# Operands of the delta-rule recurrence made by VectorE and ScalarE, and chunk products placed ahead of the bonus and the pending group norm

## The chip, the cores and the metric

The kernel runs on one core of a Trainium2 chip. The metric is the device time of one execution in microseconds, as the median of its runs. Engines are called PE (TensorE, matmuls), DVE (VectorE), ACT (ScalarE), POOL (GpSimd) and SP (SyncE, which here only issues DMAs). One execution is profiled, and its trace gives each instruction's engine, line, start and duration, and the clock that PE was granted.

## What is computed

One inference step of a hybrid decoder layer, for a prompt of 512 tokens and 8 samples of 4 tokens (together 544 columns), width 2048, in fp32. One input projection feeds three branches: RWKV-7 time mixing with 16 heads of 64, sparse attention over selected keys, and attention into 256 memory tokens. Each branch is gated, and one output projection follows. The change is inside the first branch:

```python
kk = hd(k * k_k)
kk = kk / jnp.maximum(jnp.sqrt(jnp.sum(kk * kk, axis=-1, keepdims=True)), 1e-12)
k = hd(k * (1.0 + (a - 1.0) * k_a))
def step(S, inp):
    r_t, k_t, v_t, w_t, kk_t, a_t = inp
    sa = jnp.einsum('bhvk,bhk->bhv', S, -kk_t)
    S = (S * w_t[:, :, None, :] + sa[..., None] * (kk_t * a_t)[:, :, None, :]
         + v_t[..., None] * k_t[:, :, None, :])
    return S, jnp.einsum('bhvk,bhk->bhv', S, r_t)
S_fin, y = lax.scan(step, wkv0, (r, k, v, decay, kk, a))
y = group_norm(y) * gn_w + gn_b
y = y + jnp.sum(r * k * r_k, axis=-1, keepdims=True) * v
```

Here `decay` and `a` come from two small products (w2, a2), and the last line is the bonus.

## The kernel before, in words

**The whole.** After an RMSNorm the input projection runs as fp32 split in two: each weight block is DMAed by SP (`raw`), ACT makes its rounded high half `wh` (L345) and DVE the rest `wl` (L348), and each product is three matmuls into `ps_acc`, two with `wh` and one with `wl`. These matmuls, 272 columns each, are also the filler that keeps PE busy. Attention comes before and in between. The four groups of the recurrence follow, then the output projection with its own split (L1668, L1669) and the final norm.

**The order of the work.** The kernel is written with priority levels: the recurrence at the main level, the projections of the next group's r, k and v and the gates at a level called "late", side work as "fill". A list scheduler fixes the order of every engine's queue beforehand. On the chip every engine takes its queue in order, so an instruction that waits holds all that stand behind it. The next group's projection is evacuated from PSUM by ACT (L431), DVE (L432) and ACT's copies of a last column (L435, L442), with the token shift applied; `ps_acc` has three buffers. PSUM tags `ps_ts` (tags "tp" and "sc", three buffers), `ps_L` and `ps_c` (one each) serve the recurrence.

**One group** (`rwkv_group`, L1173) holds four heads as two tiles j of 128 rows, each with two halves h of 64. It goes through these stages:

1. *Operands*, for each j (L1194 to L1236): w2 is split in two (ACT L1197, POOL L1198), multiplied (`ps_ts<-wah,w2h` and so on), evacuated (DVE L1206), and put through a sigmoid of three ACT operations (L447 to L449). DVE's scan (L1208) makes the cumulated decay CS; ACT makes PT, SG and CS by exponentials (L1209, L1211, L1212), with POOL's subtraction L1210 between; POOL copies the chunk decays DEC and DS (L1213, L1214). The keys are normalised by a matmul with a block of ones (L1219, DVE L1220, ACT L1221 and L1222, DVE L1223), and L1224, L1225 (DVE) and L1226 (POOL) make the updated key and a·kk. Last, `put` (L1143 for the prompt's 512 columns, L1144 for the samples' 32) writes the products KK·SG, AV·CS and XK·CS on DVE and XR·PT on POOL into the operand tiles LB and BK. In the profile these are called `slots` or `late`, after the pool of 2 KB slots that they lie in.
2. *Bonus* (L1238 to L1246): r·k·r_k (DVE L1241), a matmul with the block of ones into `ps_L`, the product with v (DVE L1245), a DMA to DRAM (`bd`).
3. *Pending norm* (`norm`, L1525 to L1549): the group norm of the group before. Four DVE passes over 128x1024 (L1530, L1531, L1533, L1536), a square and small activations on ACT, transposes, ACT L1544 and four DMAs (`yd`).
4. *Chunk products* (L1255 to L1279): eight times four matmuls BK by LB into `ps_ts`; ACT copies a part (MBT, L1263), DVE masks two (L1264, L1266). SP carries MBT's blocks to DRAM (`md`, L1270) and back in another layout (MB, L1283).
5. *Inversion* (L1287 to L1296): 31 steps of two DVE operations (L1291, L1293) on MB and VB, then a DMA to DRAM (`vd`) and back (TT, L1365). Meanwhile POOL does the samples' own small inversion (`mds`, L1303 to L1316) and scales BK by the chunk decays (L1324, 128x1024 for each j), and PE transposes v and BK (ACT copies L1336, L1346 and on).
6. L1375 transposes 32x32 blocks of TT on DVE, small products complete the inverse, and eight chunks run one after the other (L1468 to L1519).

Of the kernel before, what the change touches and what calls it, by code (L numbers as in the profile page):

```python
# [11 lines left out]
F32 = mybir.dt.float32  # L12
# [5 lines left out]
AF = mybir.ActivationFunctionType  # L18
# [105 lines left out]
def emit(ctx, tc, A):  # L124
# [1021 lines left out]
    def part(t, i, r=slice(0, 128)):  # L1146

        return (t[r, :1024].rearrange("p (n a t) -> p n a t", n=NCH, a=2)[:, :, i],
                t[r, 1024:].rearrange("p (a t) -> p a t", a=2)[:, i])
# [23 lines left out]
    def rwkv_group(g, pending, XK, XV, XR):  # L1173
# [17 lines left out]
        for j in range(2):  # L1191
# [6 lines left out]
            pool.tensor_tensor(W2S[1], w, W2S[0].bitcast(F32), op=OP.subtract)  # L1198
# [11 lines left out]
            pool.tensor_tensor(SG, CS, SG, op=OP.subtract)  # L1210
            act.activation(SG, SG, AF.Exp, scale=-C0)  # L1211
            act.activation(CS, CS, AF.Exp, scale=C0)  # L1212
            pool.tensor_copy(DEC[:, j], PT[:, 63:NPR:64])  # L1213
            pool.tensor_copy(DS[:, j], PT[:, NPR + NT4 - 1:NT:NT4])  # L1214
# [11 lines left out]
            pool.tensor_tensor(AV, AV, KK, op=OP.mult)  # L1226
# [6 lines left out]
            put(XR[:, j], PT, [(HS[h], *part(lb[h], 1, HS[h]), pool) for h in range(2)])  # L1233
# [3 lines left out]

        RK = R([P, 2, NT], name="rk")  # L1238
        bonus = []
        for j in range(2):  # L1240
            dve.scalar_tensor_tensor(RK[:, j], XR[:, j], vec("r_k", 2 * g + j), XK[:, j], op0=OP.mult, op1=OP.mult)  # L1241
            for t0, t1 in HV:
                ps = PS([P, 512], "L")
                bonus.append(mm(ps[:, :t1 - t0], T["bones"], RK[:, j, t0:t1]))
                dve.tensor_tensor(XK[:, j, t0:t1], ps[:, :t1 - t0], XV[:, j, t0:t1], op=OP.mult)  # L1245
        nc.sync.dma_start(BD[g * 256:(g + 1) * 256].rearrange("(j p) t -> p j t", p=P), XK)  # L1246
        F(XK, XR, RK)
        pending()

# [32 lines left out]
        for q in range(2):  # L1282
            nc.sync.dma_start(MB[HS[q]].rearrange("p s t -> p (s t)"), md)  # L1283
        pool.memset(VB, 0.0)
# [37 lines left out]
        for j in range(2):  # L1322
            b4 = BK[j][:, :1024].rearrange("p (n x) -> p n x", n=NCH)
            pool.tensor_tensor(b4, b4, DEC[:, j, :, None].to_broadcast([P, NCH, P]), op=OP.mult)  # L1324
            for a in range(2):
                bs = BK[j][:, 1024 + a * 32:1024 + (a + 1) * 32].rearrange("p (b t) -> p b t", t=NT4)
                pool.tensor_tensor(bs, bs, DS[:, j, :, None].to_broadcast([P, NB, NT4]), op=OP.mult)
# [432 lines left out]
```

## Time and profile before

| what | value |
|---|---|
| median of 3 runs | 1637.25 us (1631.7, 1637.25, 1659.45) |
| the profiled execution | 1635.43 us, span 1633.4 us |
| granted PE clock, mean | 0.967 of full |
| busy: PE, DVE, ACT, POOL | 1538.8, 960.2, 657.4, 400.0 us |
| DMA | 208.19 MB, mean 127 GB/s |
| operand stages to last sample product, groups 0 to 3 | 45.4, 58.8, 58.3, 58.3 us |
| from there to the first L1375, groups 0 to 3 | 46.4, 47.5, 43.3, 50.7 us |

The span is the time from the first to the last instruction of the profile; the execution is 2 us longer. A row of a group of instructions has the line, the engine, the operation, output and inputs with their shapes, the count, then busy time and mean time of one, and the idle time just before with what ended it ("<-ACT lc L435": ACT's instruction of line 435 that wrote `lc`). A stretch has its length, the busy time of each engine, PE's granted clock, the DMA engines' share and GB/s. In a wait, "PE ps_ts L221 <- DVE late L1144: 4.9, 1, 4.9" means that a matmul writing `ps_ts` waited in total 4.9 us, once, for DVE's L1144. All matmuls have the line of their helper, L221 (transposes L227), so they are told apart by tiles.

### The profile page before, as it was taken

To read this page: it belongs to the slowest core of one execution; us is meant where nothing else is said; L and a number is where in the kernel's file an instruction comes from. 1 tells how busy PE (TensorE), PEld (TensorE's weight loads), DVE (VectorE), ACT (ScalarE), POOL (GpSimd) and SP (SyncE) were. 2 spreads that over 40 slices of the span, in tenths; PEclk is the share of its full clock that TensorE was granted. 3 is DMA by queue.
4 is the path that set the end of the run, shared out by engine and by line. 5 is a ranking of instruction groups with operands and counts; after the bars stand their busy time and mean duration, and the time that the engine had idled before them with its cause. 6 is when DMAs were issued, how large, how long until landed. Compare 5 with 4: busy or idle time off the path is not lost. (4 is left out here: it accounts for less than half of the span.)

```text
span 1633.4 us, 31473 instructions
## 1 busy us (share of the span) xinstructions
PE 1538.8 (94%) x12011; PEld 1316.5 (81%) x12011; DVE 960.2 (59%) x2655; ACT 657.4 (40%) x1429; POOL 400.0 (24%) x542
## 2 busy tenths in 40 slices
PE   8999999789888999999999899989998999899997
PEld 6999955789888975678988798879887988777775
DVE  7746677988565642256637763676368645723333
ACT  7556643222133433244335343534353433522223
POOL 0010121120554536224032402241224113201110
PEclk9999999999999999998989898989999999999999
DMA  8733232322786756653412341134213564572233
GB/s 287 218 101 78 75 112 61 93 72 66 227 293 204 232 186 200 204 192 86 111 35 57 79 116 48 49 82 109 58 49 100 140 165 118 162 242 78 84 97 136
DMA packets 241307, 208.19 MB, mean 127 GB/s; under 512 B 45058, under 2 KB 199874, under 8 KB 241156
## 3 DMA queue, kind: packets, MB, share of 16 engines
q1 hardware_dynamic: 227460, 160.03, 34.4%
q0 software_dynamic: 13696, 46.15, 8.9%
q8 instruction: 95, 1.56, 0.4%
q14 instruction: 56, 0.46, 0.1%
HBM read 181.93 MB, written 24.19 MB: 126 GB/s over the span
## 5 line engine op out<-in xcount | busy, mean ns | idle before, releaser
L221 PE MATMUL ps_acc<-xt,wh 128*128 128x272 f32 (+1 forms) x4224 | 873.4, 299 | 13.0 <-ACT lc L435 12.1
L221 PEld LDWEIGHTS ps_acc<-xt,wh 128*128 128x128 f32 (+1 forms) x4224 | 689.0, 192 | 38.3 <-issue 13.9
L221 PE MATMUL ps_acc<-xt,wl 128*128 128x272 f32 (+1 forms) x2112 | 627.9, 297 | 3.0 <-DVE wl L348 3.0
L221 PEld LDWEIGHTS ps_acc<-xt,wl 128*128 128x128 f32 (+1 forms) x2112 | 406.4, 192 | 11.6 <-DVE wl L348 3.9
L345 ACT ACTIVATE wh<-raw 128x512 fp32r<-128x512 f32 (+1 forms) x296 | 185.4, 627 | 312.6 <-PE ps_acc L221 298.1
L348 DVE TENSOR_TENSOR wl<-raw,wh 128x512 fp32r<-128x512 f32 (+1 forms) x285 | 204.6, 719 | 143.3 <-ACT wh L345 142.4
L1669 DVE TENSOR_TENSOR wl<-raw,wh 128x512 fp32r<-128x512 f32 x58 | 43.0, 741 | 108.8 <-ACT wh L1668 97.2
L1668 ACT ACTIVATE wh<-raw 128x512 fp32r<-128x512 f32 x58 | 36.6, 630 | 116.9 <-PE ps_c L221 109.8
L221 PE MATMUL ps_acc<-wh,yt 128*128 128x512 f32 x192 | 63.3, 411 | 3.1 <-DVE late L843 3.1
L470 POOL TENSOR_TENSOR sw<-sw,slots 128x272 f32<-128x272 f32 (+1 forms) x18 | 14.0, 777 | 187.0 <-ACT sw L468 187.0
L221 PEld LDWEIGHTS ps_acc<-wh,yt 128*128 128x128 f32 x192 | 36.3, 193 | 17.5 <-ACT wh L1668 5.9
L221 PE MATMUL ps_ts<-wh,yt 128*128 128x512 f32 x156 | 50.3, 402 | 0.0
L221 PE MATMUL ps_acc<-mt,wh 128*128 128x256 f32 x256 | 48.5, 286 | 0.0
L1620 POOL TENSOR_TENSOR slots<-slots,slots 128x512 f32<-128x512 f32 x11 | 15.3, 1422 | 130.8 <-ACT tm L1618 130.8
L880 POOL DMA_INDIRECT slots<-ck,gix x36 | 37.0, 1028 | 37.3 <-DVE slots L897 22.2
L221 PEld LDWEIGHTS ps_acc<-mt,wh 128*128 128x128 f32 x256 | 40.0, 189 | 0.0
L880 POOL DMA_INDIRECT slots<-cv,gix x32 | 30.5, 954 | 36.7 <-PE ps_L L221 16.0
L221 PE MATMUL ps_ts<-slots,slots 32*32 32x32 f32 (+9 forms) x284 | 38.6, 294 | 0.6 <-DVE slots L739 0.4
L221 PE MATMUL ps_acc<-wl,yt 128*128 128x512 f32 x96 | 38.3, 399 | 0.9 <-DVE wl L1669 0.9
L221 PEld LDWEIGHTS ps_ts<-wh,yt 128*128 128x128 f32 x156 | 28.7, 188 | 12.1 <-ACT wh L1668 5.0
L221 PE MATMUL ps_acc<-mt,wl 128*128 128x256 f32 x128 | 36.7, 287 | 0.4 <-DVE wl L348 0.4
L221 PE MATMUL ps_c<-wh,yt 128*128 128x512 f32 x116 | 37.0, 399 | 0.0
(568 smaller groups left out, 2632.7 us busy)
## 6 DMA issues: line engine op xcount, KB each, us to landing
raw<-w_in SPq DMA_DIRECT2D x260, 256.0 KB, 2.9
raw<-w_out SPq DMA_DIRECT2D x64, 256.0 KB, 3.8
raw<-w_mem SPq DMA_DIRECT2D x32, 256.0 KB, 4.0
slots<-xp SPq DMA_DIRECT2D x16, 512.0 KB, 6.7
slots<-qd POOLq DMA_DIRECT2D x8, 512.0 KB, 5.6
late<-qd POOLq DMA_DIRECT2D x8, 512.0 KB, 6.0
o_y<-slots SPq DMA_DIRECT2D x8, 512.0 KB, 3.5
slots<-yd SPq DMA_DIRECT2D x7, 544.0 KB, 4.0
```

The source lines that it names most:

```text
L221: return pe.matmul(out, lhsT=lhsT, rhs=rhs, start=start, stop=stop, **kw)
L345: splits.append(act.activation(wh[:, :, :m], raw[:, :, :m], AF.Copy))
L348: eng.tensor_tensor(wl[:, :, :m], raw[:, :, :m], wh[:, :, :m].bitcast(F32), op=OP.subtract)
L470: pool.tensor_tensor(sw[:np_], sw[:np_], sin[:np_, t0:t1], op=OP.mult)
L880: pool.indirect_dma_start(out=dst[:, u], out_offset=None, in_=src, in_offset=bass.IndirectOffsetOnAxis(ap=GIX[:, 2 * q + u:2 * q + u + 1], ...
L1620: pool.tensor_tensor(z, z, nw[g // 2][:, g % 2 * 512:(g % 2 + 1) * 512], op=OP.mult)
L1668: act.activation(wh, raw, AF.Copy)
L1669: dve.tensor_tensor(wl, raw, wh.bitcast(F32), op=OP.subtract)
```

## The change

It has four parts. (1) Operations of the operand stage go from POOL to DVE: w2's low half (L1198), L1210, L1226, and the XR·PT put. (2) The two small copies DEC and DS go from POOL to ACT. (3) The bonus and the call of the pending norm move from before the chunk products to behind the issue of the MB loads; the bonus matmuls take turns in `ps_L` and `ps_c`, where they all had `ps_L`. VB's memsets follow them. (4) The scaling of BK by the chunk decay goes from one POOL operation on 128x1024 for each j to eight ACT activations on 128x128, each with its chunk's decay as a per-row scale (L1323 of the changed kernel). Lines from L1238 to L1270 move up or down by the shift: the product's copy and masks L1263, L1264, L1266 become L1250, L1251, L1253, the bonus L1241 and L1245 become L1274 and L1278, L1324 becomes L1323, and the lines behind, L1375 and the norm among them, lose 1.

```diff
--- before.py
+++ after.py
@@ -1195,7 +1195,7 @@
             W2S = [S([P, P], F32R, tag="w2" + t, bufs=1) for t in "hl"]
             w = W2A2[:, j * P:(j + 1) * P]
             act.activation(W2S[0], w, AF.Copy)
-            pool.tensor_tensor(W2S[1], w, W2S[0].bitcast(F32), op=OP.subtract)
+            dve.tensor_tensor(W2S[1], w, W2S[0].bitcast(F32), op=OP.subtract)
             SG, AV, CS, PT, KK, RN = t1[:, 0], t1[:, 1], t2[:, 0], t2[:, 1], t3[:, 0], t3[:, 1]
             for t0, t1_ in HV:
                 pss = [PS([P, 512], "sc") for _ in range(2)]
@@ -1207,11 +1207,11 @@
             sigmoid_(flat(t1))
             dve.tensor_tensor_scan(CS, T["scanm"], SG, 0.0, op0=OP.mult, op1=OP.add)
             act.activation(PT, CS, AF.Exp, scale=-C0)
-            pool.tensor_tensor(SG, CS, SG, op=OP.subtract)
+            dve.tensor_tensor(SG, CS, SG, op=OP.subtract)
             act.activation(SG, SG, AF.Exp, scale=-C0)
             act.activation(CS, CS, AF.Exp, scale=C0)
-            pool.tensor_copy(DEC[:, j], PT[:, 63:NPR:64])
-            pool.tensor_copy(DS[:, j], PT[:, NPR + NT4 - 1:NT:NT4])
+            act.copy(DEC[:, j], PT[:, 63:NPR:64])
+            act.copy(DS[:, j], PT[:, NPR + NT4 - 1:NT:NT4])
 
             act.activation(RN, XK[:, j], AF.Square, scale=vec("k_k", c))
             for t0, t1_ in HV:
@@ -1223,30 +1223,17 @@
             dve.scalar_tensor_tensor(KK, XK[:, j], vec("k_k", c), RN, op0=OP.mult, op1=OP.mult)
             dve.tensor_scalar(RN, AV, vec("k_a", c), OMKA[:, c:c + 1], op0=OP.mult, op1=OP.add)
             dve.tensor_tensor(XK[:, j], XK[:, j], RN, op=OP.mult)
-            pool.tensor_tensor(AV, AV, KK, op=OP.mult)
+            dve.tensor_tensor(AV, AV, KK, op=OP.mult)
 
             lb = [R([P, 1088], name="lb") for _ in range(2)]
             bk = R([P, 1088], name="bk")
             put(KK, SG, [(HS[h], *part(lb[h], 0, HS[h]), dve) for h in range(2)])
             put(AV, CS, [(slice(0, 128), *part(bk, 0), dve)])
             put(XK[:, j], CS, [(slice(0, 128), *part(bk, 1), dve)])
-            put(XR[:, j], PT, [(HS[h], *part(lb[h], 1, HS[h]), pool) for h in range(2)])
+            put(XR[:, j], PT, [(HS[h], *part(lb[h], 1, HS[h]), dve) for h in range(2)])
             F(t1, t2, t3)
             LB.append(lb)
             BK.append(bk)
-
-        RK = R([P, 2, NT], name="rk")
-        bonus = []
-        for j in range(2):
-            dve.scalar_tensor_tensor(RK[:, j], XR[:, j], vec("r_k", 2 * g + j), XK[:, j], op0=OP.mult, op1=OP.mult)
-            for t0, t1 in HV:
-                ps = PS([P, 512], "L")
-                bonus.append(mm(ps[:, :t1 - t0], T["bones"], RK[:, j, t0:t1]))
-                dve.tensor_tensor(XK[:, j, t0:t1], ps[:, :t1 - t0], XV[:, j, t0:t1], op=OP.mult)
-        nc.sync.dma_start(BD[g * 256:(g + 1) * 256].rearrange("(j p) t -> p j t", p=P), XK)
-        F(XK, XR, RK)
-        pending()
-
 
         AB = R([P, 2, NCH, 64], name="ab")
         MBT = R([P, 2, NCH, 64], name="mbt")
@@ -1281,6 +1268,17 @@
         MB, VB = R([P, 32, 32], name="mb"), R([P, 16, 32], name="vb")
         for q in range(2):
             nc.sync.dma_start(MB[HS[q]].rearrange("p s t -> p (s t)"), md)
+
+        RK = R([P, 2, NT], name="rk")
+        for j in range(2):
+            dve.scalar_tensor_tensor(RK[:, j], XR[:, j], vec("r_k", 2 * g + j), XK[:, j], op0=OP.mult, op1=OP.mult)
+            for (t0, t1), tag in zip(HV, "Lc"):
+                ps = PS([P, 512], tag)
+                mm(ps[:, :t1 - t0], T["bones"], RK[:, j, t0:t1])
+                dve.tensor_tensor(XK[:, j, t0:t1], ps[:, :t1 - t0], XV[:, j, t0:t1], op=OP.mult)
+        nc.sync.dma_start(BD[g * 256:(g + 1) * 256].rearrange("(j p) t -> p j t", p=P), XK)
+        F(XK, XR, RK)
+        pending()
         pool.memset(VB, 0.0)
         for q in range(2):
             pool.memset(fv(VB[HS[q]], [[34, 16]], q), -1.0)
@@ -1320,8 +1318,9 @@
 
 
         for j in range(2):
-            b4 = BK[j][:, :1024].rearrange("p (n x) -> p n x", n=NCH)
-            pool.tensor_tensor(b4, b4, DEC[:, j, :, None].to_broadcast([P, NCH, P]), op=OP.mult)
+            for n in range(NCH):
+                b = BK[j][:, n * P:(n + 1) * P]
+                act.activation(b, b, AF.Copy, scale=DEC[:, j, n:n + 1])
             for a in range(2):
                 bs = BK[j][:, 1024 + a * 32:1024 + (a + 1) * 32].rearrange("p (b t) -> p b t", t=NT4)
                 pool.tensor_tensor(bs, bs, DS[:, j, :, None].to_broadcast([P, NB, NT4]), op=OP.mult)
```

The order of three queues, in group 1. First DVE, just ahead of the first chunk product's masks, before (L1241 and L1245 are the bonus, L1533 and L1536 the norm, L348 the fill weights' split, L847 a gate):

```order
L1241 SCALAR_TENSOR_TENSOR late_2643<-slots_73,vecs,slots_72 128x544
L1245 TENSOR_TENSOR slots_72<-ps_L,slots_74 128x272
L847 TENSOR_TENSOR slots_72<-slots_72 128x544
L1245 TENSOR_TENSOR slots_72<-ps_L,slots_74 128x272
L348 TENSOR_TENSOR wl<-raw,wh 128x512
L1533 TENSOR_REDUCE gst<-late_2643 128x16
L1536 TENSOR_TENSOR slots_74<-slots_74,gst 128x1024
L348 TENSOR_TENSOR wl<-raw,wh 128x512
L1264 TENSOR_TENSOR slots_72<-ps_ts,cmain 64x256
L1266 TENSOR_TENSOR late_2643<-ps_ts,cmain 64x512
```

And in the changed kernel, around the first product's masks (L1251, L1253), with the second tile's operands from L1208 on:

```order
L432 SCALAR_TENSOR_TENSOR slots_74<-sst,vecs,slots_74 128x8
L348 TENSOR_TENSOR wl<-raw,wh 128x512
L1220 TENSOR_SCALAR late_2642<-ps_ts 128x272 x2
L1251 TENSOR_TENSOR slots_73<-ps_ts,cmain 64x256
L1253 TENSOR_TENSOR late_2643<-ps_ts,cmain 64x512
L1274 SCALAR_TENSOR_TENSOR late_2642<-slots_74,vecs,slots_72 128x544
L1198 TENSOR_TENSOR w2l<-sw,w2h 128x128
L1208 SCALAR_TENSOR_TENSOR slots_74<-cmain,late_2642 128x544
L348 TENSOR_TENSOR wl<-raw,wh 128x512
L1210 TENSOR_TENSOR late_2642<-slots_74,late_2642 128x544
L1223 SCALAR_TENSOR_TENSOR late_2642<-slots_72,vecs,late_2642 128x544
L1143 TENSOR_TENSOR late_2643<-slots_74 64x8x64
```

Bonus and norm stand ahead of the masks before; in the changed kernel only L1274 of the first tile is near them, behind the masks, and L1198 and L1210 have joined the queue. The second tile's operands now come after the first tile's first product.

Next, ACT in the changed kernel, among the copies of the chunk products (L1250):

```order
L1250 COPY late_2642<-ps_ts 64x256 x2
L1323 ACTIVATE slots_73<-slots_73,dec 128x128 x3
L1250 COPY late_2642<-ps_ts 64x256
L1323 ACTIVATE slots_73<-slots_73,dec 128x128 x2
L1250 COPY late_2642<-ps_ts 64x256
L345 ACTIVATE wh<-raw 128x512
L1323 ACTIVATE slots_73<-slots_73,dec 128x128
L1250 COPY late_2642<-ps_ts 64x256
L1323 ACTIVATE slots_73<-slots_73,dec 128x128 x2
L1323 ACTIVATE slots_72<-slots_72,dec 128x128 x3
L1250 COPY late_2642<-ps_ts 64x256
L1323 ACTIVATE slots_72<-slots_72,dec 128x128 x5
```

The decay activations (L1323) stand between the copies, eleven of the sixteen ahead of the last copy; before, the eight copies (L1263) stood in one run, and the decay was on POOL's queue.

Last, SP, before (`md` and MB are the block matrices' way to DRAM and back, `mds` the samples'):

```order
L1246 DMA bd<-slots_72 128x2x544
L360 DMA raw<-w_in 128x4x128 x2
L1549 DMA yd<-slots_73 64x512 x4
L1270 DMA md<-slots_73 32x16x32 x4
L360 DMA raw<-w_in 128x4x128
L1303 DMA mds<-atc 32x4x4
L1283 DMA late_2642<-md 64x1024 x2
```

And in the changed kernel:

```order
L1257 DMA md<-late_2642 32x16x32 x2
L360 DMA raw<-w_in 128x4x128
L1257 DMA md<-late_2642 32x16x32 x2
L360 DMA raw<-w_in 128x4x128
L1270 DMA slots_73<-md 64x1024 x2
L360 DMA raw<-w_in 128x4x128
L1279 DMA bd<-slots_72 128x2x544
L360 DMA raw<-w_in 128x4x128
L1548 DMA yd<-slots_74 64x512 x4
L1301 DMA mds<-atc 32x4x4
```

The loads from `md` (64x1024) now stand ahead of `bd`, `yd` and the first `mds`, where they stood behind all three.

## The prediction

> **What bounds the kernel now.** I read the page's busy shares first, then the busy time by stretch, then what TensorE (PE) waits for, then the granted clock, then the rows of VectorE (DVE) and GpSimd (POOL) in one group.
>
> ```profile
> PE 1538.8 (94%) x12011; PEld 1316.5 (81%) x12011; DVE 960.2 (59%) x2655; ACT 657.4 (40%) x1429; POOL 400.0 (24%) x542
> ```
>
> PE is busy 94% of the span. The change takes no work from it, so what can be won is time in which PE stands still or runs at a lower clock, in the stretches that the change touches. These are the operand stages of the four groups: from the first w2 matmul to the last product of the sample chunk.
>
> ```profile
> 717.06:762.50 45.44, 40.37 (x245) 35.20 (x244) 39.93 (x67) 22.71 (x38) 21.45 (x27) 0.89 0.27 78
> 873.57:932.40 58.83, 51.58 (x343) 45.98 (x340) 49.97 (x82) 26.91 (x51) 22.56 (x27) 0.91 0.26 70
> 1044.30:1102.60 58.30, 51.00 (x334) 46.02 (x330) 48.14 (x79) 27.57 (x49) 22.67 (x27) 0.91 0.26 70
> 1205.75:1264.00 58.25, 51.34 (x347) 46.39 (x343) 51.46 (x84) 27.91 (x52) 23.16 (x26) 0.94 0.31 84
> sum 220.82, PE 194.29 PEld 173.59 DVE 189.50 ACT 105.10 POOL 89.83; mean PE 48.57 PEld 43.40 DVE 47.38 ACT 26.27 POOL 22.46
> ```
>
> The columns are length, then busy time of PE, its weight loads, DVE, ACT and POOL, then the granted clock. PE idles 220.82 - 194.29 = 26.5 us in the four, while DVE is busy 189.5 of 220.8 and POOL at its densest. The waits of PE over this part of the program (717 to 1320 us; in total, times, longest) name the releasers:
>
> ```profile
> PE ps_acc L221 <- ACT lc L435: 8.8, 3, 4.3
> PE ps_ts L221 <- DVE late L1144: 4.9, 1, 4.9
> PE ps_ts L221 <- DVE slots L1375: 4.0, 2, 2.4
> PE ps_L L221 <- DVE slots L1245: 3.8, 1, 3.8
> PE ps_acc L221 <- DVE wl L348: 3.0, 3, 1.4
> PE ps_L L221 <- DVE late L1241: 2.6, 2, 1.6
> PE ps_L L221 <- DVE slots L1241: 2.4, 2, 1.7
> PE ps_acc L221 <- DVE slots L843: 0.9, 1, 0.9
> ```
>
> All but L1375, of which more below, end in the operand stages, and they add up to 26.4 us. L435 looks like an ACT wait, but its own row says that it stood behind DVE:
>
> ```profile
> 906.63 0.16 ACT L435 COPY lc<-ps_acc 128x1 f32<-128x1 f32 x1 [4.19 <-DVE slots L432]
> ```
>
> So one queue, DVE's, is behind every stall: the projection's evacuation (L432), its weight split (L348) and the bonus (L1241, L1245) stand in line with the operands (L1143, L1144), and PE's filler work waits with them.
>
> The stalls cost a second time. Around each the clock is granted at half:
>
> ```profile
> 736.90:747.10 10.20, 10.20 (x40) 8.81 (x40) 8.50 (x11) 4.99 (x9) 9.29 (x13) 0.50 0.19 51
> 904.20:914.40 10.20, 6.91 (x25) 6.13 (x26) 8.40 (x18) 1.86 (x5) 5.22 (x5) 0.50 0.21 56
> 1071.40:1074.80 3.40, 3.40 (x18) 3.40 (x17) 3.39 (x5) 1.56 (x3) 3.32 (x5) 0.51 0.31 82
> 1081.70:1088.50 6.80, 6.00 (x22) 5.53 (x23) 4.08 (x7) 3.54 (x6) 0.00 (x0) 0.50 0.45 151
> 1231.90:1238.70 6.80, 5.88 (x26) 5.89 (x27) 6.76 (x13) 2.57 (x7) 5.56 (x7) 0.50 0.33 80
> 907.46 0.66 PE L221 MATMUL ps_acc<-xt,wh 128*128 128x272 f32 x2
> 908.14 0.66 PE L221 MATMUL ps_acc<-xt,wh 128*128 128x272 f32 x2
> 946.16 0.41 PE L221 MATMUL ps_acc<-xt,wh 128*128 128x272 f32 x2
> 946.53 0.42 PE L221 MATMUL ps_acc<-xt,wh 128*128 128x272 f32 x2
> ```
>
> A triple of fill matmuls recurs every 0.68 us at half clock and every 0.37 us at full clock, so 46% of PE's busy time there is loss. The five periods hold 10.20 + 6.91 + 3.40 + 6.00 + 5.88 = 32.4 us of it: about 14.8 us. Ceiling of the gain in these stages: 26.5 + 14.8 = 41 us.
>
> **The change part by part.**
>
> *Operands from POOL to DVE.* First rows of group 1's operand stage (busy, then mean ns), then rows of single lines over the whole span (shortest, median and longest ns):
>
> ```profile
> L348 DVE TENSOR_TENSOR wl<-raw,wh 128x512 fp32r<-128x512 f32 x10 | 8.0, 798 | 0.7 <-ACT wh L345 0.6
> L1225 DVE TENSOR_TENSOR slots<-slots,late 128x544 f32<-128x544 f32 x2 | 1.4, 717 | 0.0
> L1143 DVE TENSOR_TENSOR slots<-late 64x512 f32<-64x512 f32 x1 | 0.7, 689 | 0.0
> L1226 POOL TENSOR_TENSOR late<-late 128x544 f32<-128x544 f32 x1 | 2.3, 2343 | 0.4 <-DVE late L1224 0.4
> L1210 POOL TENSOR_TENSOR late<-slots,late 128x544 f32<-128x544 f32 x1 | 1.8, 1799 | 2.0 <-DVE slots L1208 2.0
> L1144 DVE TENSOR_TENSOR late<-late,slots x6: 177/183/1272, 735.7 to 1241.9; 128x32 f32<-128x32 f32 x3, 64x32 f32<-64x32 f32 x3
> L432 DVE SCALAR_TENSOR_TENSOR slots<-lc,vecs,slots x17: 202/220/1318, 700.8 to 1233.5; 128x1 f32<-128x1 f32 x17
> L1224 DVE TENSOR_SCALAR late<-slots,vecs,omka x2: 540/1021/1502, 886.3 to 1056.0; 128x544 f32<-128x544 f32 x2
> L1241 DVE SCALAR_TENSOR_TENSOR slots<-slots,vecs,slots x4: 771/842/1799, 737.7 to 910.4; 128x544 f32<-128x544 f32 x4
> ```
>
> What DVE gets, per group: L1210 and L1226 for two tiles, 4 x 0.72 (L1225's row, same shape) = 2.9; the XR·PT puts, 4 x 0.69 + 4 x 0.18 (L1143, L1144) = 3.5; two w2 lows of 128 columns, at most 0.3 each (an estimate: under half of L1143's time for a quarter of its columns) = 0.6. Sum 7.0 us.
>
> What it may lose: the same L1144 takes 0.18 us, or 1.27 beside a POOL operation. The excess of the longest instance over the shortest is 1.1 for L1144, 1.1 for L432, 1.0 for L1224 and 1.0 for L1241; L348 in group 1 lies 0.11 over L1143's time for the same width, ten times: 1.1. That is 5.3 us for one instance of each in a group, and 7.5 with a second L1144 and a second L432. If POOL causes them, the bill is 7.0 - 7.5, about zero; if not, +7.0 per group. I take zero and keep both ends. The Trainium skill, "SBUF — State Buffer", section "SBUF: two separate sides", says that DVE and GpSimd share a port pair under an exclusive lock, held for a whole instruction, where the DVE operation reads two SBUF tensors; by that rule the long instances vanish with POOL's operations. L1144's 0.18 and 1.27 us agree; L1224, one tensor beside per-channel vectors, is lengthened too.
>
> The hop itself also goes: L1210 on POOL is 1.8 us against 0.72, L1226 2.3 against 0.72, both on the chain that ends at the puts. Per tile that is 2.7 us of latency at these rows, which nothing else covers when the put is what PE waits for (L1144, 4.9 us).
>
> *Bonus and pending norm behind the products.* Ahead of the first product, DVE's queue loses two L1241 (0.77 each), four L1245 and the norm's passes over 1024 columns:
>
> ```profile
> L1245 DVE TENSOR_TENSOR slots<-ps_L,slots x12: 422/440/442, 740.5 to 1085.9; 128x272 f32<-128x272 f32 x12
> L1536 DVE TENSOR_TENSOR slots<-slots,gst 128x1024 f32<-128x1024 f32 x1 | 1.2, 1224 | 0.0
> ```
>
> The norm has four passes like this one, of which two to four stood ahead of the products: 2.4 to 4.9 us. With 2 x 0.77 + 4 x 0.44 = 3.3 of bonus, the queue is 5.7 to 8.2 us shorter, against stalls of 26.4 / 4 = 6.6 us per group. PE's two bonus waits (L1245, L1241; 8.8 us in all) have no place left ahead of the products. What is late next is the operands themselves: the sigmoid and exponentials on ACT stay in the chain, with three activations between w2's evacuation and the scan, and DVE now has less to do while it waits for them. The w2 matmuls of the second tile, too, now wait on DVE, whose low half of w2 is queued behind the first tile's evacuation. I leave 1.4 us of stall per group, a fifth of 6.6: 26.5 - 5.5 = 21 us saved. The moved work is hidden by the block matrices' trip through DRAM, for which DVE's inversion waits; without that cover it would cost the inversion the same 5.7 to 8.2 us per group.
>
> *Half clock.* If stalls shrink to a microsecond, most of the half-clock time should go, but a short stall may still bring it:
>
> ```profile
> 818.90:832.60 13.70, 13.70 (x114) 11.14 (x112) 2.90 (x9) 2.74 (x10) 3.50 (x6) 0.50 0.08 20
> ```
>
> Here, ten microseconds after group 0's stall at L1375, PE ran at half clock for 13.7 us without a gap. So I keep a quarter of the loss, one group's worth: 11 us saved. The Trainium skill, "TensorE: Matmul & The Clock Gate", section "Part 1: The HAM clock gate", has the rate halved only after an idle window of about 3.4 us; by that rule all 14.8 us would go, and the sum would be 1602. The row above speaks against it.
>
> *Decay from POOL to ACT, copies to ACT.* Per group 16 activations 128x128 in place of two POOL operations on 128x1024:
>
> ```profile
> L1197 ACT ACTIVATE w2h<-sw x8: 292/309/311, 387.0 to 1208.8; 128x128 fp32r<-128x128 f32 x8
> 1264.00:1314.70 50.70, 47.88 (x384) 46.05 (x383) 32.63 (x94) 20.96 (x41) 6.25 (x16) 1.00 0.56 143
> ```
>
> 16 x 0.30 = 4.8 us per group of ACT, which the stages above show half idle (27 of 58 us). Some 11 of the 16 are queued ahead of the last product copy, and that copy starts the md DMA and so the inversion: up to 3 us later, with the weight splits (L345) waiting in the same queue. On the other side, SP now issues the MB loads ahead of bd, yd and (in groups 0 to 2) mds, where before the load stood behind mds, which waits for L1301: some 3 us earlier. So about nothing in groups 0 to 2; without the idle time of ACT it would be 3 us in each. Both figures are estimates: 11 x 0.30, and the order of SP's queue with the time from md to MB in group 1, below.
>
> ```profile
> 932.59 0.84 SPq L1270 DMA_DIRECT2D md<-slots  x2
> 938.27 1.12 SPq L1283 DMA_DIRECT2D late<-md  x2
> ```
>
> The load follows md by 5.7 us.
>
> *Where a stall goes.* The inversion chain (last product to L1375) is DVE and DMA latency and doesn't shrink. L1375 already ends a PE stall in groups 0 and 3 (4.0 us in two). In group 3 SP keeps mds ahead of MB, and fewer fill matmuls stand in the stretch (291 against 331, at 0.37 / 3 us each: 5 us less cover): PE gets there earlier. I add 3 us, between none and 5.
>
> **Sum**, against the profiled execution's 1635.4 us (1.8 under the median of 1637.25): 1635.4 - 21 - 11 + 3 = 1606 us.
>
> **The rivals.**
>
> *Everything hides (A).* DVE's queue is short enough that no operand stall is left, the half clock goes wholly, and the earlier MB load removes the L1375 stalls of 4.0 us too: 1635.4 - 41 - 4 = 1590. For it: queue 5.7 to 8.2 us shorter against 6.6. Against it: ACT's chain.
>
> *The wait moves to the inversion (B).* The products end 8 us earlier per group, ACT's decay holds the last copy back by 3 us, and PE runs out of fills before L1375: four stalls of 4 us in place of the 3 us that I added, 1606 + 16 - 3 = 1619, and 2 us for half clock after one of them: 1621. Against it: PE is busy 47.88 of 50.70 us there, with DVE at 32.63.
>
> *The queue stays as long (C).* Evacuation and weight splits still stand behind operand rows; two thirds of the stalls stay, all of the half clock, and the 3 us at the inversion and as much from ACT's decay come on top: 1635.4 - 9 + 3 + 3 = 1632. The change then doesn't do what it says: DVE's order is altered, but not its length ahead of the products.
>
> *Slower (D).* POOL isn't what lengthens the DVE rows, so DVE carries 7.0 us more per group, and the operand chain, which it now runs alone, ends later by that at the first product. It decides when the shortening by the reorder (5.7 to 8.2) is hidden behind the operands anyway: then each group's stall grows by 7.0, and half clock, at a loss of 46%, lasts as much longer: 4 x 7.0 x 1.46 = 41, so 1676. Against it: DVE's long rows coincide with POOL's.
>
> **How the numbers follow.** Forecast 0.50 at 1606, its own range 1597 to 1617; A 0.22; B 0.15; C 0.08; D 0.05. About 2%, 32.7 us, is what a measurement of this kernel tells from no change: faster lies below 1604.5, slower above 1670. Faster is A and two fifths to a half of the forecast, 0.44; slower is D, 0.05; the rest, 0.51, is within 2%. The range leaves out D, most of C and A's lowest part: 1586 to 1628.
>
> **What would show it.** Right: in the operand stages PE's waits on L435, L348 and the bonus fall from 26.4 to under 8 us; half-clock periods there fall from 37 us to under 12; DVE's rows L1144 and L432 stay near 0.2 us; L1210 and L1226 read 0.7 us on DVE. Wrong: PE waits for the puts or the product copies as long as before (C, D), or L1374 (L1375 before) ends stalls of 4 us in every group (B); DVE rows of 1.3 us beside an idle POOL would be D's sign.

## The result, and the profile after

The changed kernel takes 1592.18 us, median of 4 runs (1591.27 to 1594.3). The kernel before took 1634.47 us, median of 4 runs, beside it. The ratio is 0.973, 95% interval 0.9702 to 0.9758. The profiled execution took 1591.27 us, 44.2 us less than that of before. The forecast was 1606 with a range of 1586 to 1628: the time lies inside the range, and the forecast gain was a third too small (29.4 us against 44.2).

The page's busy times of the changed kernel:

```profile
PE 1519.9 (96%) x12011; PEld 1302.0 (82%) x12011; DVE 956.0 (60%) x2711; ACT 678.9 (43%) x1509; POOL 308.5 (19%) x462
```

PE does the same 12011 matmuls in 18.9 us less (1538.8 before), with the clock at half for some 56 us of the span where it was some 108 (its mean is 0.982 of full, 0.967 before). Its idle time is 1589.5 - 1519.9 = 69.6 us, where it was 1633.4 - 1538.8 = 94.6: 25.0 us less. The two make the 43.9 us by which the span is shorter.

The operand stages of groups 0 to 3, from the first w2 matmul to the last sample product, with the columns as before:

```profile
715.01:757.20 42.19, 40.91 (x291) 36.28 (x290) 38.64 (x79) 29.47 (x60) 2.21 (x7) 1.00 0.32 86
861.96:908.90 46.94, 46.62 (x337) 41.93 (x333) 44.54 (x93) 29.25 (x64) 1.18 (x5) 1.00 0.27 67
1014.18:1058.70 44.52, 43.46 (x317) 38.72 (x314) 42.08 (x87) 29.30 (x61) 1.59 (x8) 1.00 0.25 61
1163.08:1209.60 46.52, 46.16 (x333) 41.55 (x329) 43.92 (x91) 28.82 (x62) 1.18 (x5) 1.00 0.26 61
sum 180.17, PE 177.15 PEld 158.48 DVE 169.18 ACT 116.84 POOL 6.15; mean PE 44.29 PEld 39.62 DVE 42.30 ACT 29.21 POOL 1.54
```

220.82 us have become 180.17. PE's idle time there is 3.0 us (26.5 before), the clock is full throughout in this execution (a second one, under the experiments, has some 14 us at half there), and POOL, busy for 89.8 us before, does 6.2. What PE still waits for, from 715 to 1270 us:

```profile
PE ps_ts L221 <- DVE late L1374: 2.6, 1, 2.6
PE ps_ts L221 <- DVE slots L1143: 2.1, 5, 1.0
PE ps_c L221 <- ACT sas L1496: 1.0, 3, 0.4
PE ps_ts L221 <- DVE slots L1374: 0.6, 1, 0.6
PE ps_ts L221 <- DVE slots L1220: 0.5, 1, 0.5
```

The waits on L435, L348, L843 and the bonus are gone. The puts (L1143) hold the products up for 2.1 us in five places, and the inversion (L1374) for 3.2 in two, where it was 4.0. The single lines (shortest, median and longest ns) show the operands' new prices:

```profile
L1144 DVE TENSOR_TENSOR slots<-slots,late x10: 173/184/190, 729.1 to 1049.2; 64x32 f32<-64x32 f32 x6, 128x32 f32<-128x32 f32 x4
L432 DVE SCALAR_TENSOR_TENSOR slots<-lc,vecs,slots x18: 202/219/223, 780.6 to 1193.0; 128x1 f32<-128x1 f32 x18
L1224 DVE TENSOR_SCALAR late<-slots,vecs,omka x2: 540/549/558, 874.9 to 1173.7; 128x544 f32<-128x544 f32 x2
L1210 DVE TENSOR_TENSOR late<-slots,late x4: 714/716/717, 725.5 to 1186.1; 128x544 f32<-128x544 f32 x4
L1198 DVE TENSOR_TENSOR w2l<-sw,w2h x7: 270/281/317, 718.9 to 1167.9; 128x128 fp32r<-128x128 f32 x7
L1323 ACT ACTIVATE slots<-slots,dec x48: 384/387/403, 754.3 to 1209.2; 128x128 f32<-128x128 f32 x48
```

Before, the longest L1144, L432 and L1224 were 1.27, 1.32 and 1.50 us; none is long now. L1210 and L1198 cost on DVE what the working said (0.72, 0.28). L1323 takes 0.39 us, not 0.30: 6.2 us per group on ACT.

### The profile page after: what moved, and what is told of

Same layout as the page of the kernel before. It is cut to its first block, busy times and chain, and to the rows that moved or that the text cites. A ratio compares the mean times of both kernels' runs of the same rounds, so it can differ in the third digit from the quotient of the medians.

```text
span 1589.5 us, 31524 instructions
## 1 busy us (share of the span) xinstructions
PE 1519.9 (96%) x12011; PEld 1302.0 (82%) x12011; DVE 956.0 (60%) x2711; ACT 678.9 (43%) x1509; POOL 308.5 (19%) x462
## 4 chain that ended last, share of the span: by engine, by line
PE 59%; issue 14%; DVE 12%; DMA 7%; ACT 4%; POOL 3%; SPq 0%; POOLq 0%; ACTq 0%; DVEq 0%
PE ps_acc L221 30%; PE ps_ts L221 14%; PE ps_c L221 7%; PE ps_L L221 5%; DVE wl L348 2%; DMA late<-qd 2%; PE ps_ts L227 2%; POOL sw L470 1%; ACT wh L345 1%; DVE late L897 1%; PE ps_ts L307 1%; DMA slots<-gd 1%; DMA slots<-qd 1%; DVE slots L1143 1%; DVE slots L897 1%
## 5 line engine op out<-in xcount | busy, mean ns | idle before, releaser
L221 PE MATMUL ps_acc<-xt,wh 128*128 128x272 f32 (+1 forms) x4224 | 863.8, 296 | 5.5 <-DVE slots L843 2.9
L348 DVE TENSOR_TENSOR wl<-raw,wh 128x512 fp32r<-128x512 f32 (+1 forms) x285 | 200.0, 702 | 134.5 <-ACT wh L345 133.3
L221 PE MATMUL ps_ts<-slots,slots 32*32 32x32 f32 (+8 forms) x316 | 37.3, 270 | 2.0 <-DVE slots L1143 1.6
```

The lines of the kernel that those rows point to most:

```text
L221: return pe.matmul(out, lhsT=lhsT, rhs=rhs, start=start, stop=stop, **kw)
L348: eng.tensor_tensor(wl[:, :, :m], raw[:, :, :m], wh[:, :, :m].bitcast(F32), op=OP.subtract)
```

## The experiments

They ran on two chips. On the one the kernel before took 1666 us; on the other, where "engines, gates held back", "norm alone", "bonus alone" and "changed, again" ran, it took 1663. In the profiles from both, group 0 begins some 22 to 37 us later (w2's first matmul at 739 to 752 us), and the groups themselves are alike. So times are compared as ratios to the kernel before beside them. What the profiles are compared by is the *stretch* from w2's first matmul to the first small product behind L1375, summed over the four groups, and the fill matmuls that PE did in it. A fill takes about 0.125 us at full clock (a triple recurs every 0.37 to 0.38 us), so the stretch less 0.125 us per fill is the time the recurrence cost PE, idle and half-clock time with it.

The ratios come from 4 to 10 executions, the other columns from the one that was profiled, which need not be a typical one: against the median it took 10 us more for the engines alone, 10 less for L1210 with L1226, 15 less for the bonus alone behind, 7 less for the memsets, and 6 more for the changed kernel again.

| kernel | stretches, us | fills in them | beside fills, us | fills left behind them | ratio (95%) |
|---|---|---|---|---|---|
| before | 408.6 | 2068 | 150 | 509 | 1 |
| changed | 354.0 | 1955 | 110 | 607 | 0.973 (0.970 to 0.976) |
| changed, again | 361.1 | 1955 | 117 | 607 | 0.974 (0.965 to 0.983) |
| engines alone | 407.3 | 2264 | 124 | 308 | 0.997 (0.994 to 1.000) |
| engines, gates held back | 404.0 | 2072 | 145 | 500 | 0.996 (0.992 to 1.000) |
| order alone | 393.3 | 1949 | 150 | 631 | 0.998 (0.994 to 1.001) |
| useless products on POOL | 404.4 | 1955 | 160 | 607 | 1.010 (1.006 to 1.014) |
| memsets on POOL | 354.6 | 1955 | 110 | 607 | 0.977 (0.975 to 0.980) |
| decay back on POOL | 354.0 | 1955 | 110 | 607 | 0.976 (0.970 to 0.981) |
| L1210, L1226 back on POOL | 370.9 | 1931 | 130 | 616 | 0.992 (0.988 to 0.995) |
| more on DVE | 388.4 | 2039 | 134 | 522 | 0.989 (0.985 to 0.994) |
| norm alone behind | 375.0 | 2066 | 117 | 501 | 0.979 (0.972 to 0.986) |
| bonus alone behind | 383.8 | 2182 | 111 | 376 | 0.984 (0.977 to 0.991) |
| MB first | 353.3 | 1955 | 109 | 607 | 0.978 (0.974 to 0.981) |

**The engines alone.** The kernel before with part (1) and the two copies of part (2):

```diff
-            pool.tensor_tensor(SG, CS, SG, op=OP.subtract)
+            dve.tensor_tensor(SG, CS, SG, op=OP.subtract)
...
-            pool.tensor_tensor(AV, AV, KK, op=OP.mult)
+            dve.tensor_tensor(AV, AV, KK, op=OP.mult)
...
-            put(XR[:, j], PT, [(HS[h], *part(lb[h], 1, HS[h]), pool) for h in range(2)])
+            put(XR[:, j], PT, [(HS[h], *part(lb[h], 1, HS[h]), dve) for h in range(2)])
```

> The kernel before with the change of engines alone in the operand stage (w2's low half, L1210, L1226, the XR·PT put to VectorE, the two small copies to ScalarE); the bonus and the pending norm stay ahead of the chunk products and the decay stays on GpSimd. Theory (both parts are needed: the VectorE queue ahead of the products is shortened about equally by the contention that goes and by the bonus and norm that move behind): VectorE gets 7.0 us per group and loses about 7.5 us of lengthened rows, the two hops go, the stalls in the operand stages fall from 26.4 to some 12 us: about 1615 us. Rival 1 (the order alone does it): within 5 us of before, 1630 to 1640. Rival 2 (the engines alone do it): about 1595.

Measured: 0.997. The theory, 1615 us or half of the gain, fell, and the result is rival 1's. Yet PE's stalls did shrink. The sum row of the four stretches (length, busy times), first of the kernel before:

```profile
sum 408.60, PE 376.16 PEld 348.67 DVE 314.03 ACT 184.28 POOL 115.39; mean PE 94.04 PEld 87.17 DVE 78.51 ACT 46.07 POOL 28.85
```

And of the engines alone:

```profile
sum 407.30, PE 392.64 PEld 364.58 DVE 313.32 ACT 196.15 POOL 41.40; mean PE 98.16 PEld 91.15 DVE 78.33 ACT 49.04 POOL 10.35
```

PE idles 407.30 - 392.64 = 14.7 us in them, where it idled 408.60 - 376.16 = 32.4. The stretches aren't shorter, though: they hold 2264 fills in place of 2068. And at the end, where the fills are missing, the same kernel shows this wait (from 1400 us on):

```profile
PE ps_L L221 <- DMA raw<-w_out: 20.8, 1, 20.8
```

**The order alone.** The changed kernel with operands, copies and decay on POOL:

```diff
-            dve.tensor_tensor(SG, CS, SG, op=OP.subtract)
+            pool.tensor_tensor(SG, CS, SG, op=OP.subtract)
...
-                b = BK[j][:, n * P:(n + 1) * P]
-                act.activation(b, b, AF.Copy, scale=DEC[:, j, n:n + 1])
+            b4 = BK[j][:, :1024].rearrange("p (n x) -> p n x", n=NCH)
+            pool.tensor_tensor(b4, b4, DEC[:, j, :, None].to_broadcast([P, NCH, P]), op=OP.mult)
```

> The changed kernel with the operand work, the copies and the decay back on GpSimd: only the order is changed (bonus and pending norm behind the chunk products and the MB loads). Theory (both parts are needed): the queue is 5.7 to 8.2 us shorter ahead of the products, but the lengthened VectorE rows and the hops of 1.8 and 2.3 us stay: stalls of some 12 us left and half of the half-clock time: about 1612 us. Rival 1 (the order alone does it): about 1595. Rival 2 (the engines alone do it): 1628 to 1636.

Measured: 0.9976, nothing either. The theory fell, and neither rival's pair (one run near 1595, the other near 1635) came. The waits of PE, 740 to 1329 us:

```profile
PE ps_ts L221 <- DVE slots L1143: 5.3, 2, 4.0
PE ps_ts L221 <- DVE late L1144: 5.0, 1, 5.0
PE ps_acc L221 <- ACT lc L435: 4.1, 2, 2.4
PE ps_ts L221 <- DVE late L1143: 4.0, 1, 4.0
PE ps_ts L221 <- POOL late L1143: 3.9, 2, 2.4
PE ps_ts L221 <- POOL slots L1143: 2.6, 2, 1.3
```

No wait is on the bonus, and 20.8 us are on the puts, of which 4.9 were seen before. The products moved ahead, and found their operands not made: POOL's hops and DVE's long rows (26.7 us above their shortest times, by the sum that is explained under "POOL beside DVE") were still in front.

**Engines, with gates held back.** To see whether the engines alone had gained in the stages and lost it at the end, two gates were moved to group 3, so that 500 fills stayed for the end. A gate here is the projection of 128 columns of the branches' gates, fill work of 96 matmuls, and GCUT deals the 16 of them to the four groups:

```diff
-    GCUT = (0, 3, 4, 6, 16)
+    GCUT = (0, 2, 3, 4, 16)
```

> The change of engines alone (as in the first run of that kind), with the gates dealt to the groups as (2, 1, 1, 12) in place of (3, 1, 2, 10), so that 500 fill matmuls are left behind group 3's first small product where the engines alone left 308 (before: 509; the changed kernel: 607). Theory (the engines alone do speed up the operand stages, and gave it back at the end, where the fills had run out and TensorE waited 20.8 us for the first weights of the output projection): that wait is gone, the four stretches from w2 to the first small product stay near 124 us beside their fills, ratio 0.982 to 0.988. Rival (the additional fills were what covered the stalls): the stretches go back to some 140 us or more beside their fills, ratio 0.993 to 1.000.

Measured: 0.996, the rival's. The wait for w_out is gone, and the stalls are back in the stages, 145 us beside the fills. They are back where the fills were taken: groups 1 and 2, with 470 fills in place of 566, went from 29.8 and 30.2 us beside them to 43.1 and 42.9, while groups 0 and 3 kept their fills and stand at 28.7 and 30.3. What PE waits for in group 1 (894 to 997 us), and the clock from the longest of these waits on:

```profile
PE ps_ts L227 <- DVE slots L1536: 4.2, 1, 4.2
PE ps_L L221 <- DVE slots L1245: 2.5, 3, 1.5
PE ps_L L221 <- DVE slots L1241: 1.2, 1, 1.2
PE ps_ts L227 <- DVE slots L1266: 1.1, 1, 1.1
PE ps_acc L221 <- ACT lc L435: 1.0, 1, 1.0
```

```profile
935.10:959.00 23.90, 22.14 (x118) 20.66 (x119) 10.67 (x21) 9.57 (x27) 6.87 (x14) 0.50 0.24 55
```

Here the waits are the bonus's and the norm's, and no put is among them; over all four groups they are 18.2 us (L1536 8.5, L1245 5.1, L1241 4.6) against 0.5 on the puts. With the order alone it was the other way round. So two chains stand ahead of the products side by side: the operands by POOL, and the bonus (four times PE to DVE through one `ps_L`) with the norm, whose transposes stand ahead of the products in PE's queue. With either one left, the four stretches take 393 to 407 us, hardly less than with both, 408.6; with neither, 354.0. Each hid the other.

**POOL beside DVE.** Useless work on POOL behind each tile's scan, in the changed kernel; the queues of PE, DVE, ACT and SP are the changed kernel's:

```diff
+            dum = S([P, 512], tag="tm", bufs=2)
+            pool.tensor_copy(dum[:, 0:1], CS[:, 0:1])
+            for _ in range(4):
+                pool.tensor_tensor(dum, XR[:, j, :512], T["scanm"][:, :512], op=OP.mult)
```

> The changed kernel with useless work on GpSimd: behind each tile's scan a copy of one column and four products 128x512 of two SBUF tiles into a scratch tile that nobody reads; the order of all other engines is unchanged. Theory (GpSimd's operations lengthen VectorE's rows): rows like L1144, L432 and L1224 show instances of 1.3 to 1.8 us again, some 5 to 7 us more per group, and part of the stalls and of the half clock come back: 1605 to 1620 us. Rival (the long rows had another cause): VectorE's rows stay at their short times and the run stays at 1592 us within 3.

The second run has memsets in place of the products:

```diff
-            for _ in range(4):
-                pool.tensor_tensor(dum, XR[:, j, :512], T["scanm"][:, :512], op=OP.mult)
+            for _ in range(10):
+                pool.memset(dum, 0.0)
```

> As the run with useless products on GpSimd, but with ten memsets of 128x512 per tile in place of the four products: GpSimd is busy as long and only writes. If any GpSimd operation that touches SBUF lengthens VectorE's rows, it comes out like the products, 1605 to 1620 us; if only those that read SBUF do, it stays at 1592 us within 3, with VectorE's rows at their short times.

Measured: 1.010 with the products, 1% above the kernel before; 0.977 with the memsets, 0.004 above the changed kernel with the same stretches. The products cost 3.3 to 3.7% or 54 to 62 us, by the run with memsets or by the changed kernel's ratio (the changed kernel itself didn't run on this chip). That is well above the theory's 13 to 28; the direction is the theory's. The rows with the products:

```profile
L1144 DVE TENSOR_TENSOR slots<-slots,late x10: 175/186/1282, 768.0 to 1114.9; 64x32 f32<-64x32 f32 x6, 128x32 f32<-128x32 f32 x4
L1144 DVE TENSOR_TENSOR late<-slots,late x5: 176/181/1284, 931.9 to 1103.8; 64x32 f32<-64x32 f32 x4, 128x32 f32<-128x32 f32 x1
...
L1215 POOL TENSOR_TENSOR tm<-slots,cmain x32: 1270/1668/3182, 760.2 to 1282.6; 128x512 f32<-128x512 f32 x32
```

And with the memsets:

```profile
L1144 DVE TENSOR_TENSOR slots<-slots,late x10: 174/184/191, 764.3 to 1085.1; 64x32 f32<-64x32 f32 x6, 128x32 f32<-128x32 f32 x4
L1144 DVE TENSOR_TENSOR late<-slots,late x5: 174/181/185, 915.2 to 1075.2; 64x32 f32<-64x32 f32 x4, 128x32 f32<-128x32 f32 x1
...
L1215 POOL MEMSET tm<- x80: 518/527/1117, 760.5 to 1226.1; 128x512 f32 x80
```

Adding up every DVE instance's time above the shortest of its line and shape, where it is over 0.25 us, in the first 62 us of each group: 30.9 us in 31 instances before, all of them while a POOL operation ran; none in the changed kernel; 28.5 us with the products; 0.7 us with the memsets, though POOL is busy with those for over 42 us. So POOL's products of two SBUF tiles lengthen these rows of DVE, and POOL operations that only write don't. The rise from 354.0 to 404.4 us in that run is put down to it: the memsets come with the same copy of a column and 44 us of POOL time against the products' 54, and their stretches stay at 354.6. The price is higher than the lengthening: 28.5 us of DVE time came to 50 us, 65 us of the stretches being at half clock, where 28 us of plain DVE work (below) came to 34 with 24 us at half clock. What makes that difference isn't shown.

**Which operations on POOL.** The decay alone, and L1210 with L1226 alone, put back on POOL in the changed kernel:

> The changed kernel with the chunk decay of BK back on GpSimd (two operations 128x1024 per group in place of sixteen activations). Theory: the decay is hidden on either engine, since the product masks that run beside it read PSUM and one SBUF tile: the masks stay at 0.42 and 0.70 us and the ratio to the kernel before stays at 0.973 within 0.005. Rival (any GpSimd product beside VectorE costs what the useless products cost): masks lengthened to over 1 us, some 8 us of stall, ratio 0.980 to 0.985.

```diff
-            for n in range(NCH):
-                b = BK[j][:, n * P:(n + 1) * P]
-                act.activation(b, b, AF.Copy, scale=DEC[:, j, n:n + 1])
+            b4 = BK[j][:, :1024].rearrange("p (n x) -> p n x", n=NCH)
+            pool.tensor_tensor(b4, b4, DEC[:, j, :, None].to_broadcast([P, NCH, P]), op=OP.mult)
```

> The changed kernel with L1210 and L1226 alone back on GpSimd (w2's low half and the XR·PT put stay on VectorE; order of the code as in the changed kernel). Theory (the operations on the chain of the operands are what keeps the products late): the two hops and the lengthened rows beside them cost 3 to 4 us per group of stall and part of the half clock: ratio 0.983 to 0.992. Rival (the number of GpSimd operations decides, not their place): half of them are back, half of the gain is left, ratio 0.986 as well, but then with the lengthened rows at the puts and not at the hops; if the order of the products alone were the cause, 0.973.

```diff
-            dve.tensor_tensor(SG, CS, SG, op=OP.subtract)
+            pool.tensor_tensor(SG, CS, SG, op=OP.subtract)
...
-            dve.tensor_tensor(AV, AV, KK, op=OP.mult)
+            pool.tensor_tensor(AV, AV, KK, op=OP.mult)
```

Measured: the decay 0.976, with the same 354.0 us, as the theory had it: moving the decay gives nothing and costs nothing that these runs can tell. The masks kept their times, though 25 of the 64 ran while the decay's products were on POOL:

```profile
L1251 DVE TENSOR_TENSOR slots<-ps_ts,cmain x24: 404/417/419, 773.2 to 1244.8; 64x256 f32<-64x256 f32 x24
L1253 DVE TENSOR_TENSOR slots<-ps_ts,cmain x16: 693/694/695, 780.7 to 1240.2; 64x512 f32<-64x512 f32 x16
L1322 POOL TENSOR_TENSOR slots<-slots,dec x6: 1896/1896/1897, 789.0 to 1244.4; 128x1024 f32<-128x1024 f32 x6
```

So not every DVE row is lengthened beside a POOL product of two SBUF tiles: those that read PSUM and one SBUF tile weren't.

L1210 and L1226 came to 0.992, within the theory's range: four operations per group, two thirds of the gain. The rival's 0.986 lies outside the interval. The lengthened rows come to 12.2 us there, mostly L1225 and L1224 next to the hop, as the theory had it. What of the loss is the hops' own latency and what these rows wasn't separated.

**More work on DVE.** Five useless products per tile on DVE, behind L1210:

```diff
+            dve.tensor_copy(dum[:, 0:1], CS[:, 0:1])
+            for _ in range(5):
+                dve.tensor_tensor(dum, XR[:, j, :512], T["scanm"][:, :512], op=OP.mult)
```

> The changed kernel with useless work on VectorE: behind each tile's L1210 five products 128x512 of two SBUF tiles, some 7 us more per group, nothing on GpSimd. It prices a longer VectorE queue by itself. Theory (the queue ahead of the products has about 1.5 us of slack per group, so some 5 us of stall per group come back with part of the half clock): 20 to 35 us over the changed kernel, ratio 0.985 to 0.994. Rival (the queue has room, and only blocking by GpSimd made the operands late): ratio 0.973 to 0.978. The slower case of the prediction (7.0 us per group cost 41 us): ratio 0.998.

Measured: 0.989, as the theory had it; the stretches grew by 34.4 us for 4 x 7 = 28 us of DVE work, of which 10.5 us are 84 more fills: 24 us beside them. The scheduler's order differs in this kernel, and the stalls come out at another place (PE's waits, 740 to 1345 us):

```profile
PE ps_acc L221 <- DVE slots L843: 11.1, 2, 6.0
PE ps_ts L227 <- DVE slots L1539: 2.5, 1, 2.5
PE ps_acc L221 <- ACT lc L435: 1.1, 1, 1.1
```

So DVE's queue has little or no slack, as far as a kernel with another order can tell.

**Norm or bonus.** One of the two ahead of the products again, the other behind. Norm behind:

```diff
+        RK = R([P, 2, NT], name="rk")
...
+        F(XK, XR, RK)
         AB = R([P, 2, NCH, 64], name="ab")
...
-        F(XK, XR, RK)
         pending()
```

> The changed kernel with the bonus ahead of the chunk products again and the pending norm behind them. Theory (what counts is VectorE's time ahead of the products): the bonus puts back 3.3 us of VectorE and two waits of TensorE per group, the norm stays away with 2.4 to 4.9: about half of the order's part is lost, ratio 0.976 to 0.983. Rival (only the bonus mattered, whose waits TensorE showed before): the whole part of the order is lost, ratio 0.984 to 0.990.

Bonus behind:

```diff
+        pending()
         AB = R([P, 2, NCH, 64], name="ab")
...
         F(XK, XR, RK)
-        pending()
```

> The changed kernel with the pending norm ahead of the chunk products again and the bonus behind them. Theory: two to four passes of 1.22 us stand ahead of the products, about half of the order's part is lost, but 374 fills are left at the end, so some of it comes out there: ratio 0.978 to 0.988. Rival (only the bonus mattered): nothing is lost in the stages, ratio 0.973 to 0.977.

Measured: 0.979 and 0.984. Each lies in its theory's range, but the intervals overlap each other and the changed kernel's, so which of the two weighs more stays open. The stretches, 375.0 and 383.8 us, lie 21 and 30 us above the changed kernel's 354.0, where both ahead (the engines alone) lie 53 above; with the norm ahead, the added time is nearly all fills (2182), and those are missing at the end. In the first of the two the bonus keeps its turns in `ps_L` and `ps_c`; what this second buffer is worth by itself was not run.

**The changed kernel again, and MB first.**

> The changed kernel itself, unchanged, beside these runs on the same chip. Expected: ratio 0.973 within 0.004, stretches of 110 us beside their fills. If it came out at 0.977 or above, the ratios of the runs on this chip would have to be read against that.

Measured: 0.974, with a wide interval (0.965 to 0.983; the four runs took 1608.7 to 1632.4 us). So this repeats the gain, but it can't tell ratios of 0.973 and 0.977 apart. The profile has one half-clock period of 17.1 us in group 0 that the first didn't have (361.1 against 354.0 us); some 14 us of it lie in the operand stage. Just ahead of it PE had waited for a put (773 to 786 us), and then it was busy without a gap:

```profile
PE ps_ts L221 <- DVE slots L1143: 1.0, 1, 1.0
785.30:802.40 17.10, 17.10 (x68) 14.50 (x69) 9.39 (x18) 7.99 (x22) 1.57 (x4) 0.50 0.16 31
```

> The changed kernel with the samples' small inversion made to wait for the load of the block matrices (one column of its tile is first written by GpSimd from MB), so that SyncE issues the MB loads ahead of the first mds store in group 3 too, where it stood behind it. Theory: the 2.6 us stall at L1374 in group 3 and most of the 20.5 us at half clock behind it go: 5 to 11 us less than the changed kernel, ratio 0.967 to 0.970. Rival (half clock in the small products comes without a stall): 0 to 3 us less, ratio 0.971 to 0.973.

```diff
+        pool.tensor_copy(atc[:, 0:1], MB[0:32, 0, 0:1])
         dve.tensor_reduce(tb(atc), ats[0:32].rearrange("p h j (c t) -> p (h j) t c", t=NT4)[:, :, :, 0:8], AX.X, OP.add)
```

Measured: 0.978 (0.974 to 0.981), no gain; the rival's 0.971 to 0.973 isn't reached either. The stall at L1374 in group 3 fell from 2.6 to 1.5 us. Half clock came at other small products instead, 13.7 us in group 0 and 10.2 in group 2, without a stall of 1 us ahead of them. That needn't come from the edit: the changed kernel itself has 3.4, 3.4, 3.4 and 20.5 us of it behind the stretches of the four groups in one profile and 3.4, 10.2, 6.8 and 10.2 in the other. So there isn't a version here that beats the changed kernel.

## Why the prediction was right

The time, 1592, lies in the stated range, but below the forecast's own 1597 to 1617. It is nearest to rival A's 1590, which had a chance of 0.22. What bounds the kernel was read rightly. That the sum came near is in part luck: it credits the saved idle time to the reorder alone, and the runs show that the reorder alone saves next to nothing.

- *The bound.* Right: PE's idle and half-clock time in the operand stages was what could be won, and it went. Forecast ceiling 41 us, found 23.5 us of idle time (26.5 to 3.0) and, in the profiled execution, the whole 14.8 us of half clock; the other 5.9 us of the 44.2 lie outside these stages. By the stretches it is the same: 54.6 us shorter, 14.1 of them 113 fills that PE does later, 40.5 beside the fills.
- *Idle time.* Its size was near: 5.5 us were to stay, 3.0 did, so what was late next cost less than the 1.4 us per group that were left for it. The account of where it comes from was not right (see the queue, below).
- *Half clock.* A quarter of the loss was kept. In the profiled execution nothing stayed in these stages: 11 us forecast, 14.8 found, the largest miss of the sum; the 18.9 us that PE's busy time lost also hold periods elsewhere in the program. In the second profile of the same kernel a wait of 1.0 us was followed by 17.1 us at half clock, a cost of some 7 us, so the reserve for a short stall was a fair one. The rule of the Trainium skill that was weighed there ("TensorE: Matmul & The Clock Gate", section "Part 1: The HAM clock gate", sum 1602) is the nearer one for the first profile and doesn't cover the second, where no wait of 3.4 us stood ahead of the half clock.
- *The 3 us at the inversion* didn't come: L1374 ends 3.2 us of stall where L1375 ended 4.0. Rival A had the direction right, though not that all of it would go.
- *Moved operands at about zero.* As DVE's bill this is right, and shown: DVE's long rows were 30.9 us in four groups, 7.7 each, against the estimated 7.5, and POOL's reading operations were their cause. As the worth of the move it is wrong: L1210 and L1226 alone, put back on POOL, lose two thirds of the gain (0.992 against 0.973). The working names the hop, 2.7 us per tile, and gives it no term in the sum. The other bound, +7.0 per group at 41 us, is refuted as a case; its price, measured by more work on DVE, is 34 us in the stretches, 24 of them beside the fills, and 0.989 against 0.974 in time.
- *The queue as one sum.* Here the reasoning was too simple. The forecast took the bonus and norm (5.7 to 8.2 us) from one DVE queue as if the stalls shrank with it, and set the moved operands at zero; by that, the reorder alone should have given most of the gain. The runs show two chains side by side: each part alone gives 0.2 to 0.4%, hardly clear of none, both 2.7%. The total came out near because both were changed at once.
- *Rival C* (the queue stays as long) is near to what the order alone does, but not for its reason: it named evacuation and weight splits behind operand rows, and there PE waited 4.1 us on L435 and 20.8 us for the puts themselves. *Rival B* didn't come.
- *Decay.* Rightly costed at nothing, though one activation takes 0.39 us, not 0.30.
- *Loads of MB earlier.* Overrated: from the last product mask to the inversion it is 9.0, 9.5, 10.4 and 12.3 us in the four groups, where it was 11.1, 10.7, 10.3 and 11.7 (the start of the first L1291 or L1289 less the end of the last L1266 or L1253). That is 2 us at best, not 3.

## What to carry to other kernels

Where two chains run side by side ahead of the same work, shortening either alone may show nothing; look for what would be late next before calling a change useless, and try both. Filler work on a saturated engine is a budget: a stall that is covered with it in one place can come back where it runs out, here as 20.8 us before the output projection. Half-clock time changes between executions of one kernel, here by 17.1 us in the operand and inversion stages of group 0, so one profile doesn't settle what an edit did to it. An operation given to a second engine to relieve the first must be priced with what it does to the first's neighbouring instructions.

## What the runs showed of the hardware

- A 0.18 us DVE product took up to 1.28 us beside a POOL product of two SBUF tiles and stayed at 0.18 to 0.19 beside POOL memsets. That the Trainium skill's "SBUF — State Buffer", section "SBUF: two separate sides", limits the exclusion for a two-input DVE operation to POOL operations that read agrees with both runs. DVE's masks, which read PSUM and one SBUF tile, stayed at 0.42 and 0.69 us beside POOL's decay products of 1.90 us.
- The half clock came back with stalls of about 4 us (23.9 us long with the gates held back), but also behind a wait of 1.0 us (17.1 us long, in the changed kernel's second profile) and in the changed kernel's small products. The stretch from 1256 us, behind the 2.6 us stall, has PE busy all of 21.00 us:

```profile
1256.00:1277.00 21.00, 21.00 (x208) 19.47 (x206) 5.93 (x10) 5.62 (x11) 1.04 (x1) 0.52 0.42 117
```

  The run with MB first halved that stall and had half clock in the small products of other groups. What sets it off there wasn't settled.
- The same two kernels took about 2% longer on the chips of the experiments (1663 to 1666 and 1626 us); for the changed kernel, the profiles put 36 of the 41 us ahead of group 0. The ratios agreed (0.973 and 0.974).
